# Layer 0's opening by pairs of channel tiles in column groups, with four accumulations begun inside it

## The chip, the cores and the metric

The kernel runs on one core of a Trainium2 chip. The metric is device time in microseconds, the median of three runs. Matrix products run on TensorE (PE), elementwise work on VectorE (DVE) and ScalarE (ACT). SyncE (SP) issues most transfers, ACT some of them, and both draw on the same 16 DMA engines.

## The reference, cut to what matters

The program computes two layers of a hybrid backbone (window attention, convolution and a gated recurrence side by side) over 256 context and 1024 latent tokens of width 1024. What the change touches is how layer 0 begins: the modulation vectors come from `c` and `c_ctx`, the normalised tokens are scaled and shifted by them, and the result `h` (for the context `hc`) feeds every product of the layer.

```python
for l in range(DEPTH):
    shift, scale, gate = jnp.split(jax.nn.silu(c) @ w_ada[l] + b_ada[l], 3, axis=-1)
    shift_c, scale_c, gate_c = jnp.split(jax.nn.silu(c_ctx) @ w_ada[l] + b_ada[l], 3, axis=-1)
    h = layer_norm(x) * (1.0 + scale[:, None]) + shift[:, None]
    hc = layer_norm(ctx) * (1.0 + scale_c) + shift_c
    q, k, v, g_att, u_conv, g_conv, x_lru, g_lru = split_in_proj(h @ w_in[l])
    ...
    g = jax.nn.sigmoid(h @ w_gate + b_gate)
    ...
```

## The kernel before, in words

Everything is float32. A product of tokens and weights is made as three passes: weights and tokens are each split into a high and a low part (`whi`, `wlo`, and `hchi`, `hclo` for the context, `hlhi`, `hllo` for the latent tokens), and high by high, high by low and low by high accumulate in PSUM. The tokens stand as three column groups: NT_C (256 context tokens), NT_0 and NT_1 (512 latent tokens each). The channel axis has eight tiles of 128 (`j` or `k` from 0 to 7), so one output tile of 128 columns over one token group takes 24 matmuls: eight channel tiles by three passes.

`emit_h0` makes layer 0's `h`. `load_ada` brings a 256 by 512 piece of the modulation weights; `ada_rows` multiplies it by the two conditioning vectors in `cs` (two columns of the array) into a row tile `pa`; when a group of 512 columns is complete, `ada_fin` copies it (`arow`), and four small matmuls against `sel` turn it into columns, which DVE adds to the bias in `ada[0]`. Groups 0 and 1 are the shift, 2 and 3 the scale, so the first channel tile can be modulated only when group 2 is done and the last when group 3 is done. `load_x` and `norm_x` bring ten tiles of 128 tokens and normalise them (ACT, `x<-x,nb,rs`). `modulate(j, nt)` transposes one channel tile of a token group on PE (tile `p`), scales and shifts it on ACT (`hf`), and splits it into the high and low parts on ACT and DVE. The order of the loads, row products, normalisations and modulations is a list written out by hand (`order`, line 488). `load_rows` issues eleven small loads of bias and parameter rows on SP's queue, in the middle of the first modulation weights.

After `emit_h0`, `phase1` runs the layer's streams. A planner (`Driver`) picks the next piece among nine streams by priority, with estimates of when engines and operands are free. `lru_in` multiplies `w_in` into the recurrence's input, `gates` multiplies `w_gate` into the merge gates, both through `gemm_nt`, which writes all 24 matmuls of one output tile and then evacuates it. PSUM tiles of the name `ps` come from a ring of four, counted by the pool `pl_`; `gates` may also use wide tiles from another pool, opened after the opening's own. Weights go through `wcols`: a 512 KB load on SP, a copy to `whi` on ACT, a difference to `wlo` on DVE. The compiler's scheduler then orders each engine's queue; a queue runs strictly in that order.

Of the kernel before, what the change touches and what calls it, by code (L numbers as in the profile page):

```python
# [18 lines left out]
KD = 8  # L19
# [170 lines left out]
def kernel(  # L190
# [66 lines left out]
    def load_rows(l, get):  # L257
        ra, rb = get(), get()
        dve.memset(ra[96:128], 0.0)
        dve.memset(rb[96:128], 0.0)  # L260
        for off, n, src in (
            (P_ADA, 24, b_ada[l].rearrange("(r p) -> r p", p=128)),
            (P_GATE, 24, b_gate[l].rearrange("(r p) -> r p", p=128)),
            (P_CB, 4, conv_dw_b[l].rearrange("(r p) -> r p", p=128)),
            (P_CG, 4, conv_ln_g[l].rearrange("(r p) -> r p", p=128)),
            (P_CLB, 4, conv_ln_b[l].rearrange("(r p) -> r p", p=128)),
            (P_LCW, 32, lru_conv_w[l].rearrange("d k (r p) -> (d k r) p", p=128)),
            (P_LCB, 8, lru_conv_b[l].rearrange("d (r p) -> (d r) p", p=128)),
            (P_BA, 8, lru_b_a[l].rearrange("d (r p) -> (d r) p", p=128)),
            (P_BX, 8, lru_b_x[l].rearrange("d (r p) -> (d r) p", p=128)),  # L270
            (P_LAM, 8, lru_lambda[l].rearrange("d (r p) -> (d r) p", p=128)),
        ):
            sp.dma_start(out=ra[off:off + n], in_=src)
        sp.dma_start(out=rb[0:CK * 4], in_=conv_dw_w[l].rearrange("k (r p) -> (k r) p", p=128))
        return ra, rb
# [147 lines left out]
    hT, hr = {}, {}  # L423

# [3 lines left out]

    def emit_h0(R, P):
        tiles = [(ctxt, 0), (ctxt, 128)] + [(x, 128 * i) for i in range(8)]  # L430
        raws, xt = {}, {}
        nts = (NT_C, NT_0, NT_1)

        def load_x(i):
            t = R.tile([128, 2, 512], F32, tag="raw0", name="x0", bufs=17).rearrange("p a b -> p (a b)")
# [3 lines left out]
        def load_ada(g, q):  # L439
            raws[g, q] = R.tile([128, 2, 512], F32, tag="raw0", name="raw0", bufs=17)  # L440
            sp.dma_start(out=raws[g, q], in_=w_ada[0][q * 256:q * 256 + 256, g * 512:g * 512 + 512].rearrange(
                "(k p) n -> p k n", p=128))

        rows_ = {}

        def ada_rows(g, q):
            if q == 0:
                rows_[g] = P.tile([128, 512], F32, tag="p0", name="pa", bufs=4)
            for k in range(2):
                pe.matmul(out=rows_[g][0:2], lhsT=cs[:, q * 2 + k, :], rhs=raws[g, q][:, k, :],  # L450
                          start=(q == 0 and k == 0), stop=(q == 3 and k == 1))
            if q == 3:
                ada_fin(0, [g * 4 + i for i in range(4)], rows_[g], 2,
                        R.tile([128, 512], F32, tag="hf0", name="arow", bufs=5))
# [8 lines left out]
        def modulate(j, nt):  # L463
# [5 lines left out]
            hf = R.tile([128, 512], F32, tag="hf0", name="hf0", bufs=5)  # L469
# [15 lines left out]
        def rows_tile():  # L485
            return R.tile([128, 128], F32, tag="rows", name="rows", bufs=2)

        order = [("a", 0, 0), ("a", 0, 1), ("a", 0, 2), ("r",), ("a", 2, 0), ("a", 0, 3), ("a", 2, 1), ("a", 2, 2),
                 ("a", 2, 3), ("x", 0), ("x", 1), ("a", 1, 0), ("a", 1, 1), ("a", 1, 2), ("a", 1, 3), ("a", 3, 0),
                 ("a", 3, 1), ("a", 3, 2), ("a", 3, 3), ("m", NT_C, 0), ("m", NT_C, 4), ("x", 2), ("x", 3),  # L490
                 ("x", 4), ("x", 5), ("x", 8), ("m", NT_0, 0), ("m", NT_0, 4), ("x", 6), ("x", 9), ("x", 7),
                 ("m", NT_1, 0), ("m", NT_1, 4)]
        for what, *v in order:
            if what == "m":
                for j in range(v[1], v[1] + 4):
                    modulate(j, v[0])
            elif what == "r":
                load_params(0, *load_rows(0, rows_tile))
            elif what == "a":
                load_ada(*v)  # L500
                ada_rows(*v)
            else:
                load_x(*v)
                norm_x(*v)
# [20 lines left out]
    def phase1(l, R, RH):  # L525
# [5 lines left out]
        sl, hl_, pl_ = Pool_(NS), Pool_(NHF), Pool_(4)  # L531
        state = dict(lru=False, late=False)
# [64 lines left out]
        def lru_in():  # L597
            for cc in range(4):
                yield ("pe", both(lambda: xgo[0] >= cc, wroom(), sl.room(), hl_.room(3)))
                w = wcols(w_in[l], O_XL + cc * 128)  # L600
# [18 lines left out]
                for nt in allt:  # L619
                    yield from gemm_nt(w, nt, evac)  # L620
# [482 lines left out]
        gorder = list(range(16, 24)) + list(range(8, 16)) + list(range(8))  # L1103

        def gate_nt(w, j, nt):
# [7 lines left out]
            yield from gemm_nt(w, nt, evac, wide=True)  # L1113
# [3 lines left out]
        def gates():  # L1117
            ws = {}
# [369 lines left out]
```

## Time and profile before

| what | value |
|---|---|
| time, median of 3 runs | 2296.81 us (2293.95 to 2297.31) |
| the profiled execution's own time | 2297.23 us |
| its span, first to last instruction | 2295.4 us |
| PE busy | 2246.4 us (98%) |
| DVE busy | 1680.8 us (73%) |
| ACT busy | 1005.5 us (44%) |
| mean granted clock of TensorE | 0.992 |

PE is busy nearly all the time, so a saving must come from time in which PE waits, works at its lower clock, or does work that need not be done. The views shown below are: the page's list of busy times; stretches of time with the busy time of each engine, the granted clock (1.00 is 2.4 GHz, 0.50 is 1.2 GHz) and the DMA engines' share; groups of instructions with their mean duration; instructions in order of time; and the waits of one engine.

### The profile page before, as it was taken

The page shows a single profiled execution, that of the slowest core. Times are in us where ns is not written, and L with a number is a line of the kernel's source. Part 1 is how long each engine was busy: PE and PEld are TensorE (multiplying, and loading weights), DVE is VectorE, ACT ScalarE, POOL GpSimd, SP SyncE. Part 2 cuts the span into 40 slices and gives each one's busy share as a digit, 9 for nine tenths or more (in the row PEclk, how much of TensorE's full clock was granted, in tenths as well). Part 3 has the DMA queues.
Part 4 walks back from the last instruction along what each step waited for, and adds up shares of the span by engine and source line. Part 5 has one row for each costly group of instructions (what it writes and reads, how often), then busy time and mean ns, then how long its engine had stood idle before and what let it go on. Part 6 is the DMA issues. An engine that isn't in the chain of part 4 may idle for free.

```text
span 2295.4 us, 29965 instructions
## 1 busy us (share of the span) xinstructions
PE 2246.4 (98%) x11344; PEld 1869.6 (81%) x11344; DVE 1680.8 (73%) x2453; ACT 1005.5 (44%) x1642; POOL 88.3 (4%) x140
## 2 busy tenths in 40 slices
PE   7999999999999999999999999999999999999998
PEld 2888888888888787888888888888888878878886
DVE  5579967868859875444668849879778797755667
ACT  3555563245445465421122654565343456642110
POOL 1000000000000110000001200000000011000002
PEclk8999999999999999999999999999999999999999
DMA  7223323433334233545571222224423234347532
GB/s 277 77 74 101 115 68 127 148 106 111 97 114 141 81 104 97 186 165 176 145 229 69 101 61 75 76 91 130 146 87 106 83 115 138 119 145 216 162 127 92
DMA packets 270945, 279.90 MB, mean 122 GB/s; under 512 B 19768, under 2 KB 199888, under 8 KB 270800
## 3 DMA queue, kind: packets, MB, share of 16 engines
q1 hardware_dynamic: 242288, 226.06, 32.0%
q10 hardware_dynamic: 28512, 51.92, 6.4%
q8 instruction: 89, 1.46, 0.3%
q14 instruction: 56, 0.46, 0.1%
HBM read 203.04 MB, written 74.88 MB: 121 GB/s over the span
## 4 chain that ended last, share of the span: by engine, by line
PE 91%; DVE 3%; ACT 2%; DMA 2%; issue 1%; SPq 0%; POOLq 0%; ACTq 0%; DVEq 0%
PE ps L73 84%; PE yp L73 3%; PE pt L73 2%; PE pa L73 1%; DMA raw<-in_w_ada_dram 1%; DMA yst<-yd 1%; ACT whi L73 1%; DVE acc L73 0%; DVE P L73 0%; DVE wlo L73 0%; DVE pl L73 0%; PE p L73 0%; ACT ph L73 0%; DVE gs L73 0%; ACT P L73 0%
## 5 line engine op out<-in xcount | busy, mean ns | idle before, releaser
L73 PE MATMUL ps<-hlhi,whi 128*128 128x512 f32 x1728 | 681.7, 395 | 2.5 <-DVE pl L73 1.5
L73 PE MATMUL ps<-hllo,whi 128*128 128x512 f32 x1728 | 678.0, 392 | 0.0
L73 PE MATMUL ps<-hlhi,wlo 128*128 128x512 f32 x1728 | 677.1, 392 | 0.0
L73 PEld LDWEIGHTS ps<-hlhi,wlo 128*128 128x128 f32 x1728 | 325.8, 189 | 68.1 <-issue 0.4
L73 PEld LDWEIGHTS ps<-hlhi,whi 128*128 128x128 f32 x1728 | 326.2, 189 | 66.5 <-DVE pl L73 2.6
L73 PEld LDWEIGHTS ps<-hllo,whi 128*128 128x128 f32 x1728 | 326.2, 189 | 61.9 <-issue 0.2
L73 DVE SCALAR_TENSOR_TENSOR acc<-u,cwt,acc 128x1296 f32<-128x1296 f32 (+1 forms) x240 | 341.8, 1424 | 2.2
L73 ACT ACTIVATE whi<-raw 128x1024 fp32r<-128x1024 f32 x180 | 190.1, 1058 | 342.3 <-PE ps L73 307.4
L73 DVE TENSOR_TENSOR wlo<-raw,whi 128x1024 fp32r<-128x1024 f32 x180 | 220.5, 1225 | 97.8 <-ACT whi L73 97.4
L73 PE MATMUL ps<-yy,whi 128*128 128x512 f32 (+1 forms) x960 | 271.5, 368 | 1.8 <-DVE m L73 1.8
L73 PEld LDWEIGHTS ps<-yy,whi 128*128 128x128 f32 x960 | 173.6, 188 | 32.5 <-DVE m L73 2.2
L73 PE MATMUL ps<-yy,wlo 128*128 128x512 f32 (+1 forms) x480 | 176.5, 368 | 0.0
L73 ACT ACTIVATE ph<-pt 128x512 fp32r<-128x512 f32 x160 | 94.2, 593 | 146.2 <-PE pt L73 145.6
L73 DVE TENSOR_TENSOR pl<-pt,ph 128x512 fp32r<-128x512 f32 x160 | 109.2, 685 | 60.5 <-ACT ph L73 58.9
L73 PE MATMUL ps<-hchi,whi 128*128 128x256 f32 x480 | 135.9, 283 | 1.5 <-ACT whi L73 0.8
L73 PE MATMUL ps<-hchi,wlo 128*128 128x256 f32 x480 | 135.4, 282 | 1.0 <-DVE wlo L73 1.0
L73 PE MATMUL ps<-hclo,whi 128*128 128x256 f32 x480 | 134.8, 281 | 0.0
L73 ACT ACTIVATE P<-P,nm 128x640 f32<-128x640 f32 (+1 forms) x128 | 101.9, 798 | 72.7 <-DVE nm L73 72.0
L73 DVE CUSTOM_DVE_ANT_0 P<-ps,m_mid,nsink 128x640 f32<-128x640 f32 (+1 forms) x112 | 93.5, 859 | 43.6 <-PE ps L73 42.1
L73 ACT ACTIVATE tg<-ps,drv 128x512 f32<-128x512 f32 (+1 forms) x120 | 76.5, 638 | 68.4 <-PE ps L73 67.9
L73 PEld LDWEIGHTS ps<-yy,wlo 128*128 128x128 f32 x480 | 90.4, 188 | 15.2
L73 PE MATMUL pt<-ident,P 128*128 128x128 f32 x640 | 98.0, 273 | 3.2 <-DVE pl L73 1.4
(205 smaller groups left out, 3398.4 us busy)
## 6 DMA issues: line engine op xcount, KB each, us to landing
raw<-in_w_in_dram SPq DMA_DIRECT2D x60, 512.0 KB
raw<-in_w_ada_dram SPq DMA_DIRECT2D x48, 512.0 KB
raw<-in_w_gate_dram SPq DMA_DIRECT2D x48, 512.0 KB
th<-tg ACTq DMA_DIRECT2D x96, 256.0 KB
thl<-th SPq DMA_DIRECT2D x96, 256.0 KB
yd<-gs ACTq DMA_DIRECT2D x48, 256.0 KB
yst<-yd SPq DMA_DIRECT2D x48, 256.0 KB
raw<-in_w_branch_dram SPq DMA_DIRECT2D x24, 512.0 KB
```

Of the source, the lines that this page charges most:

```text
L73: return f(*a, **k)
```

## The change

Within `emit_h0` the unit of work becomes a pair of channel tiles.

- `load_ada(g)` brings the shift and the scale columns of channel tiles 2g and 2g+1 together, as eight loads of 256 KB with contiguous pieces of 1 KB in DRAM (before: 512 KB with pieces of 2 KB).
- `ada_cols(g)` multiplies them with the conditioning vectors padded to 32 columns (`csz`). The eight channel tiles go to four column groups of the array, `k % 4`, each accumulating two of them into its own 32 partitions of `pa`. ACT copies all 128 partitions, and a matmul against `sel4` (four stacked two-column identities) adds the four partial sums and turns them into columns. The number of matmuls against modulation weights stays 32.
- The weights of the first `lru_in` tile and of the first gate tile are loaded within the opening (`first`), and four accumulations begin there: `lru` over NT_C, NT_0 and NT_1, and `gate` over NT_0. `share(j, nt)` adds channel tile `j` to them: three matmuls each. All four `ps` tiles are held until the planner's streams evacuate them (`pl_.take(4)`).
- The high part's copy is made on ACT for all modulations; before, DVE made it for 10 of 24 (channel tiles 4 to 7 of NT_C and of NT_0, and 6 and 7 of NT_1).
- The eleven small row loads go to ACT's queue.
- The buffers of `x0` and `raw0` become 18 instead of 17, `hf0` 4 instead of 5, and `arow` gets one of its own.

```diff
+        def load_ada(g):
+            for q in range(4):
+                raws[g, q] = R.tile([128, 2, 2, 256], F32, tag="raw0", name="raw0", bufs=18)
+                src = w_ada[0][q * 256:q * 256 + 256, 0:2 * D].rearrange("(k p) (t n) -> p k t n", p=128, t=2)
+                for k in range(2):
+                    sp.dma_start(out=raws[g, q][:, k], in_=src[:, k, :, g * 256:g * 256 + 256])
+        def ada_cols(g):
+            pa = P.tile([128, 512], F32, tag="p0", name="pa", bufs=4)
+            for k in range(KD):
+                c_ = k % 4
+                pe.matmul(out=pa[32 * c_:32 * c_ + 32], lhsT=csz[:, k, :],
+                          rhs=raws[g, k // 2][:, k % 2].rearrange("p t n -> p (t n)"), start=(k < 4), stop=(k >= 4),
+                          tile_position=(0, 32 * c_))
+            row = R.tile([128, 512], F32, tag="arow", name="arow", bufs=1)
+            act.activation(out=row, in_=pa, func=AF.Copy)
+            for i in range(4):
+                pe.matmul(out=pa[:, 2 * i:2 * i + 2], lhsT=row[:, i * 128:i * 128 + 128], rhs=sel4, start=True, stop=True)
...
-            if j < (4, 4, 6)[ti]:
-                act.activation(out=hi, in_=hf[:, 0:n], func=AF.Copy)
-            else:
-                dve.tensor_copy(hi, hf[:, 0:n])
+            act.activation(out=hi, in_=hf[:, 0:n], func=AF.Copy)
...
+        def share(j, nt):
+            for kind in ("lru", "gate"):
+                if (kind, nt[0]) in first:
+                    w, ps = first[kind], first[kind, nt[0]]
+                    for i, (a, b) in enumerate(((0, 0), (0, 1), (1, 0))):
+                        pe.matmul(out=ps[:, 0:nt[2]], lhsT=w[a][:, j, :], rhs=hT[0, nt[0]][b][:, j, :],
+                                  start=(j == 0 and i == 0), stop=(j == KD - 1 and i == 2))
...
+        ra, rb = load_rows(0, lambda: R.tile([128, 128], F32, tag="rows", name="rows", bufs=2), act)
+        for i in range(2):
+            load_x(i)
+        load_ada(0)
...
+        for g in range(1, 4):
+            if g < 3:
+                ada_cols(g + 1)
+            for nt in nts:
+                for j in (2 * g - 2, 2 * g - 1):
+                    share(j, nt)
+                for j in (2 * g, 2 * g + 1):
+                    modulate(j, nt)
+        for nt in nts:
+            for j in (6, 7):
+                share(j, nt)
```

What the change does to the queues is shown at three places. In the rows, `x_214` and `x_216` (before: `x_262`, `x_275`) are the context's token tiles, numbers after a name tell one buffer from another, and `128x512` is the shape written.

PE, the modulation weights. Before, the row products of one piece stand together, two columns wide, and the first transposes come behind three groups of them:

```order
L73 MATMUL pa<-raw_301,cs 2x512 x2
L73 MATMUL pa<-raw_312,cs 2x512 x2
L73 MATMUL p_336<-ident,x_262 128x128
L73 MATMUL p_336<-ident,x_275 128x128
L73 MATMUL p_343<-ident,x_262 128x128
L73 MATMUL p_343<-ident,x_275 128x128
L73 MATMUL pa<-raw_317,cs 2x512 x2
L73 MATMUL pa<-sel,arow 128x2 x4
```

Now:

```order
L73 MATMUL pa<-raw_276,csz 32x512
L73 MATMUL p_419<-ident,x_239 128x128
L73 MATMUL p_428<-ident,x_239 128x128
L73 MATMUL pa<-raw_276,csz 32x512
L73 MATMUL ps<-hchi,wlo 128x256
L73 MATMUL ps<-hchi,whi 128x256
L73 MATMUL ps<-hclo,whi 128x256
L73 MATMUL ps<-hchi,wlo 128x256
L73 MATMUL pa<-raw_279,csz 32x512
```

The matmuls of group 1 are now separated by transposes of the token tiles and by the first shares.

PE, the last modulation weights. Before, they stand ahead of nearly all transposes, and the products with `hchi` begin when those of NT_C are over:

```order
L73 MATMUL pa<-raw_321,cs 2x512 x2
L73 MATMUL pa<-raw_325,cs 2x512 x2
L73 MATMUL p_350<-ident,x_262 128x128
L73 MATMUL p_350<-ident,x_275 128x128
L73 MATMUL pa<-sel,arow 128x2 x4
```

Now they stand behind the whole share of pair 0 and one matmul of pair 1:

```order
L73 MATMUL ps<-hlhi,wlo 128x512
L73 MATMUL ps<-hchi,whi 128x256
L73 MATMUL pa<-raw_407,csz 32x512 x2
L73 MATMUL pa<-raw_410,csz 32x512 x2
L73 MATMUL pa<-raw_413,csz 32x512 x2
L73 MATMUL pa<-raw_416,csz 32x512 x2
L73 MATMUL ps<-hclo,whi 128x256
L73 MATMUL ps<-hchi,wlo 128x256
L73 MATMUL ps<-hchi,whi 128x256
L73 MATMUL p_613<-ident,x_214 128x128
```

All that is left of pair 1's share, and every transpose of pairs 2 and 3, follows the eight matmuls of group 3 in PE's queue.

SP, the transfers. Before, the parameter rows stand behind the first three pieces:

```order
L441 DMA raw_201<-in_w_ada_dram 128x2x512
L273 DMA rows<-in_b_ada_dram 24x128
L273 DMA rows<-in_b_gate_dram 24x128
L273 DMA rows<-in_conv_dw_b_dram 4x128
L273 DMA rows<-in_conv_ln_g_dram 4x128
```

Now SP's queue has none of them in the opening; at its end three weight tiles stand between or behind the last pieces:

```order
L332 DMA raw<-in_w_gate_dram 128x8x128
L449 DMA raw_364<-in_w_ada_dram 128x2x256 x2
L449 DMA raw_367<-in_w_ada_dram 128x2x256 x2
L449 DMA raw_370<-in_w_ada_dram 128x2x256 x2
L449 DMA raw_373<-in_w_ada_dram 128x2x256 x2
L449 DMA raw_407<-in_w_ada_dram 128x2x256 x2
L332 DMA raw<-in_w_gate_dram 128x8x128
L449 DMA raw_410<-in_w_ada_dram 128x2x256 x2
L449 DMA raw_413<-in_w_ada_dram 128x2x256 x2
L449 DMA raw_416<-in_w_ada_dram 128x2x256 x2
L332 DMA raw<-in_w_in_dram 128x8x128
```

The second gate tile is loaded within group 3, and the second `w_in` tile right behind it.

## Rows read from the trace of the kernel before

**Rows 1.** The page, busy time, share of the span and instructions of each engine.
```profile
PE 2246.4 (98%) x11344; PEld 1869.6 (81%) x11344; DVE 1680.8 (73%) x2453; ACT 1005.5 (44%) x1642; POOL 88.3 (4%) x140
```

**Rows 2.** Stretches (us): busy us of PE, PEld, DVE, ACT, POOL; clock, DMA share, GB/s.
```profile
6.40:41.40 35.00, 34.45 (x96) 8.80 (x96) 14.30 (x61) 5.11 (x9) 2.17 (x4) 1.00 0.96 345
41.40:55.40 14.00, 8.14 (x38) 5.62 (x38) 11.88 (x39) 14.00 (x23) 2.29 (x5) 0.62 0.47 162
55.40:58.30 2.90, 2.90 (x15) 2.71 (x14) 2.41 (x6) 2.90 (x5) 1.65 (x2) 0.50 0.70 201
58.30:74.00 15.70, 15.70 (x110) 14.22 (x110) 10.67 (x18) 15.70 (x25) 0.66 (x5) 1.00 0.24 73
...
456.00:600.00 144.00, 135.94 (x765) 115.06 (x764) 113.70 (x206) 69.99 (x145) 0.00 (x0) 0.98 0.36 106
...
790.00:930.00 140.00, 132.41 (x706) 111.15 (x705) 88.22 (x165) 87.66 (x164) 19.54 (x15) 0.96 0.29 90
```

**Rows 3.** Groups of PE's instructions by shape, 0 to 73.97 us: busy, mean ns.
```profile
L73 PE MATMUL pa<-raw,cs 128*2 128x512 f32 x64 | 30.5, 627 | 0.6 <-DMA raw<-in_w_ada_dram 0.3 <-DVE cs L73 0.3
L73 PE MATMUL p<-ident,x 128*128 128x128 f32 x80 | 15.4, 329 | 5.8 <-ACT hf L73 3.9 <-ACT x L73 1.9
L73 PE MATMUL ps<-hchi,whi 128*128 128x256 f32 x16 | 5.1, 320 | 0.0
...
L73 PE MATMUL ps<-hllo,whi 128*128 128x512 f32 x10 | 4.3, 426 | 0.0
L73 PE MATMUL pa<-sel,arow 2*128 2x2 f32 x32 | 4.2, 249 | 0.3 <-ACT arow L73 0.3
...
L73 PE MATMUL ps<-hlhi,wlo 128*128 128x512 f32 x9 | 3.5, 393 | 0.0
```

**Rows 4.** PE in order of time (start, us, operation): how closely matmuls follow each other.
```profile
14.41 7.03 PE L73 MATMUL pa<-raw,cs 128*2 128x512 f32 x16 [0.29 <-DMA raw<-in_w_ada_dram]
...
76.56 0.28 PE L73 MATMUL ps<-hchi,whi 128*128 128x256 f32 x1
...
79.38 0.39 PE L73 MATMUL ps<-hlhi,whi 128*128 128x512 f32 x1
79.61 0.39 PE L73 MATMUL ps<-hllo,whi 128*128 128x512 f32 x1
```

**Rows 5.** The chain of work that ended last, in order of time, near 70 us.
```profile
70.14 0.87 PE p L73 x8
```

**Rows 6.** SP's queue in order of time (start, us, transfers).
```profile
1.91 1.42 SPq L441 DMA_DIRECT2D raw<-in_w_ada_dram  x3
...
9.66 0.25 SPq L274 DMA_DIRECT2D rows<-in_conv_dw_w_dram  x1
```

**Rows 7.** DMA packets and rates in 8:11, 22:30, 33:37 and 39:41.5 us, in this order.
```profile
DMA packets 144, 0.05 MB, mean 18 GB/s; under 512 B 49, under 2 KB 141, under 8 KB 144
...
DMA packets 1605, 3.09 MB, mean 386 GB/s; under 512 B 96, under 2 KB 96, under 8 KB 1605
...
DMA packets 451, 1.63 MB, mean 409 GB/s; under 512 B 55, under 2 KB 55, under 8 KB 450
...
DMA packets 1433, 0.73 MB, mean 294 GB/s; under 512 B 19, under 2 KB 1430, under 8 KB 1433
```

**Rows 8.** Groups of ACT's instructions by shape, 8 to 74 us: busy, mean ns.
```profile
L73 ACT ACTIVATE hf<-p,ada 128x512 f32<-128x512 f32 x15 | 10.8, 757 | 0.0
L73 ACT ACTIVATE hlhi<-hf 128x512 fp32r<-128x512 f32 x10 | 5.8, 613 | 0.0
L73 ACT ACTIVATE whi<-raw 128x1024 fp32r<-128x1024 f32 x4 | 4.2, 1040 | 0.0
L73 ACT ACTIVATE hf<-p,ada 128x256 f32<-128x256 f32 x8 | 4.2, 542 | 0.0
...
L73 ACT ACTIVATE hchi<-hf 128x256 fp32r<-128x256 f32 x4 | 1.5, 398 | 0.0
```

**Rows 9.** Waits of PE, whole span: who waited for whom, us, times, longest.
```profile
PE yp L73 <- ACT ph L73: 7.9, 10, 2.2
```

More of the change, by code (lines that the diff above doesn't have):

```diff
@@ L423 @@
     hT, hr = {}, {}
+    GATES = list(range(16, 24)) + list(range(8, 16)) + list(range(8))
     def alloc_h(ti, n):
@@ new lines, in ada_cols @@
+        def ada_cols(g):
[9 more added lines that the diff above has]
+                pe.matmul(out=pa[:, 2 * i:2 * i + 2], lhsT=row[:, i * 128:i * 128 + 128], rhs=sel4, start=True, stop=True)
+            for part in range(2):
+                jj = 8 * part + 2 * g
+                bias = prm[0][:, P_ADA + jj:P_ADA + jj + 2].unsqueeze(2).to_broadcast([128, 2, 2])
+                dve.scalar_tensor_tensor(out=ada[0][:, jj:jj + 2, :],
+                                         in0=pa[:, 4 * part:4 * part + 4].rearrange("p (m s) -> p m s", s=2),
+                                         scalar=float(part), in1=bias, op0=ALU.add, op1=ALU.add)
@@ L483, in emit_h0 @@
                 pad(H, 64, "padh2")
[L485 to L504, printed above, removed]
+        ra, rb = load_rows(0, lambda: R.tile([128, 128], F32, tag="rows", name="rows", bufs=2), act)
+        for i in range(2):
+            load_x(i)
+        load_ada(0)
+        load_params(0, ra, rb)
+        for i in range(2, 6):
+            load_x(i)
+        for i in range(2):
+            norm_x(i)
+        first["lru"] = wcols(w_in[0], O_XL)
+        load_ada(1)
+        ada_cols(0)
+        for i in range(2, 6):
+            norm_x(i)
+        for i in range(6, 10):
+            load_x(i)
+        first["gate"] = wcols(w_gate[0], GATES[0] * 128)
+        for nt in nts:
+            first["lru", nt[0]] = psum()
+        first["gate", 1] = psum()
+        load_ada(2)
+        for nt in nts:
+            for j in (0, 1):
+                modulate(j, nt)
+            if nt is NT_C:
+                ada_cols(1)
+                load_ada(3)
+            if nt is NT_0:
+                for i in range(6, 10):
+                    norm_x(i)
+        for g in range(1, 4):
+            if g < 3:
+                ada_cols(g + 1)
+            for nt in nts:
+                for j in (2 * g - 2, 2 * g - 1):
+                    share(j, nt)
+                for j in (2 * g, 2 * g + 1):
+                    modulate(j, nt)
+        for nt in nts:
+            for j in (6, 7):
+                share(j, nt)
     class Pool_:
@@ L531, in phase1 @@
         sl, hl_, pl_ = Pool_(NS), Pool_(NHF), Pool_(4)
+        if first:
+            pl_.take(4)
         state = dict(lru=False, late=False)
@@ L598, in lru_in @@
             for cc in range(4):
-                yield ("pe", both(lambda: xgo[0] >= cc, wroom(), sl.room(), hl_.room(3)))
-                w = wcols(w_in[l], O_XL + cc * 128)
+                yield ("pe", both(lambda: xgo[0] >= cc, lambda: "lru" in first or wroom()(), sl.room(), hl_.room(3)))
+                w = first.pop("lru", None) or wcols(w_in[l], O_XL + cc * 128)
                 sl.take()
@@ L619, in lru_in @@
                 for nt in allt:
-                    yield from gemm_nt(w, nt, evac)
+                    if ("lru", nt[0]) in first:
+                        yield "act"
+                        evac(first.pop(("lru", nt[0]))[:, 0:nt[2]], nt)
+                        pl_.give()
+                    else:
+                        yield from gemm_nt(w, nt, evac)
                 w.free()
@@ L1101, in att_out @@
                 yield from gating(0, j, get, 1.0)
-        gorder = list(range(16, 24)) + list(range(8, 16)) + list(range(8))
+        gorder = GATES
         def gate_nt(w, j, nt):
@@ L1111, in evac @@
                 act.activation(out=th[:, 0:nt[2]], in_=ps, func=AF.Tanh, scale=0.5, bias=d[:, 16 + j:17 + j])
-            yield from gemm_nt(w, nt, evac, wide=True)
+            if ("gate", nt[0]) in first:
+                yield "act"
+                evac(first.pop(("gate", nt[0]))[:, 0:nt[2]], nt)
+                pl_.give()
+            else:
+                yield from gemm_nt(w, nt, evac, wide=True)
             act.dma_start(out=th_d[j][:, nt[1]:nt[1] + nt[2]], in_=th[:, 0:nt[2]])
@@ L1117, in gates @@
         def gates():
-            ws = {}
+            ws = {0: first.pop("gate")} if l == 0 else {}
             def fetch(i):
```

34 lines of the change are left out of this document (14 added, 20 removed).

## The prediction

> **What bounds the kernel now.** I read the page's busy times first. PE is busy 2246.4 us of the span [rows 1], so there is little to gain except where PE stands, runs at its lower clock, or does work that is not a product. Next I cut the span into stretches [rows 2]. From 6.4 to 41.4 us PE and the DMA engines are both full (34.45 of 35 us; share 0.96). From 41.4 to 55.4 us PE works 8.14 of 14 us, ACT all of it, and the clock's mean is 0.62. From 58.3 us on PE is full at 1.00.
>
> The question is how late the products of layer 0 start. I call **head** the moment at which the opening is over less the product time already done by then; behind it PE is full, so a shorter head shortens the run by as much, unless later gaps change. Before, the last transposes end at 73.97 us. Until then there are 48 products of 256 columns (three kinds of 16) and 29 of 512 columns (10, 10 and 9) [rows 3]. At full clock one of 256 takes 0.1175 us (24 between 76.56 and 79.38) and one of 512 takes 0.23 us [rows 4]. Done: 48 x 0.1175 + 29 x 0.23 = 12.3 us. The head is 73.97 - 12.3 = **61.7 us**.
>
> What fills it: 64 records against modulation weights (32 matmuls, two records each), 30.5 us of records [rows 3], at 7.03 / 16 = 0.44 us apiece when dense [rows 4]; 80 transposes, in which PE waits 5.8 us for ACT [rows 3]; 32 records against `sel`, 4.2 us; and the lower clock until 58.3 us [rows 2].
>
> **The change, part by part.** The accumulations begun in the opening are 24 x 0.1175 + 72 x 0.23 = 19.4 us of products, 4.85 us for each pair of channel tiles. So the new head is the new end of the opening less 19.4.
>
> *Transfers.* The opening must bring ten token tiles (5.24 MB, pieces of 4 KB), the modulation weights (8.39 MB, now pieces of 1 KB) and three weight tiles that stand ahead of the last piece in SP's queue (first `w_in`, first and second gate tile, 1.57 MB, pieces of 512 B). Pieces of 4 KB moved at 409 GB/s, of 2 KB at 386, of 512 B at 294 [rows 7]. No row shows a full stream of 1 KB pieces, so its rate is bounded by the last two; I take their middle, 340, since 1 KB lies one doubling from each. Sum: 12.8 + 24.7 + 5.3 = 42.8 us (39.8 to 46.6 by the bounds). It starts about 1 us after the first big issue at 1.91 us [rows 6], so at 2.9. The parameter rows leave SP's queue: between 8 and 11 us it moved only 18 GB/s [rows 7] while those issues ran until 9.66 us [rows 6]. That hole of about 3 us goes, but ACT's row loads now share the completion semaphores with SP, which at first has only half of them for pieces of 256 KB; I put 1.5 us back. With 1 us from the last byte to the signal the last modulation weights land at 2.9 + 1.5 + 42.8 + 1 = **48.2 us** (45 to 52).
>
> The Trainium skill says in *DMA: Bandwidth & Descriptors*, Specifications, that line rate needs pieces of at least 512 B. By that the 1 KB pieces would cost nothing against 4 KB, and the modulation weights would take 8.39 / 0.409 = 20.5 us, 4 us less. The rate of 294 GB/s at 512 B [rows 7] speaks against it, and the sum goes by the rows.
>
> *PE behind that landing.* PE's queue is strict, and by the order nearly all of pairs 1 to 3 stands behind the last eight modulation matmuls. What is left then: the last matmul's two records (0.9 us), 40 transposes at 0.87 / 8 = 0.11 us [rows 5] (4.4), eight records against `sel4` (32 took 4.2 us [rows 3], so 1.0) and three pairs of shares (14.6). That is 20.9 us: 48.2 + 20.9 = 69.1 us if PE never waits. I add 3 us for waits of transposes and shares on ACT: before it was 5.8 us with nothing else queued, and now products stand between; bounds 0 and 5.8. I add 2 us for the clock: PE waits for the last weights, and before it regained the full clock 2.9 us after products had become dense at 55.4 (clock 0.50 in 55.4:58.3, 1.00 behind it [rows 2]), which costs half of that; bounds 0 and two such spells with more. The opening ends at **74.1 us**, later than before by nothing to speak of, but with 19.4 us of products done: head 74.1 - 19.4 = **54.7 us**.
>
> *ACT, the other bound.* The new queue holds a copy to `whi` that waits for the second `w_in` tile, 1.8 us of transfer (0.52 MB at 294) behind the last modulation weights: 50 us, then 1.0 for it, and about 1.2 for two late steps. A pair is 2 x (0.54 + 0.40) + 4 x (0.76 + 0.61) = 7.4 us [rows 8], so pairs 2 and 3 end by 52.3 + 14.8 = 67.1 us. PE, at 69.1 to 74.1, is later, so the high copies that ACT takes over from DVE cost nothing; were PE's waits gone, ACT would be next, 2 us earlier.
>
> *The column groups.* At 0.44 us a record one matmul is 0.88 us, a 256 KB piece 0.77 us at 340 GB/s. One after another they lag their data by 8 x 0.11 = 0.9 us a group. Side by side they would free up to 21 us of PE, but in the stretch where PE waits for data. Between the two I take one after another for the end of group 3, and no gain elsewhere.
>
> Speaking against the change, the Trainium skill says in *TensorEngine Tiling (Array Packing)*, Key Properties, that a change of tiling mode drains TensorE. No row here shows a tiled matmul. The order shows 36 such changes in the opening, 35 of them before the last weights are through. A transpose's record lasts 0.27 us beside its 0.11 us share of the queue; if each change exposes that difference, 36 x 0.16 = 5.8 us, of which all but one lie where PE waits for data. The sum stays, but I keep the case below.
>
> *Buffers and the rest.* Group 2 reuses buffers freed by group 0 long before, group 3 those of group 1, whose matmuls are done some 6 us ahead of their issue. SP issues faster than the transfers run (three in 1.42 us [rows 6]). `csz`, `sel4` and the padded copies are a few DVE and ACT steps ahead of the first weights. These I put at nothing; their cover is the wait for the first weights.
>
> *Behind the opening.* The same products remain. The recurrence's first evacuations come earlier, so the planner starts attention earlier in PE's queue. The attention stretches lose time now: 8.1 us of PE gaps in 456:600 and 7.6 in 790:930, with clock means of 0.98 and 0.96 [rows 2], mostly products with values waiting for the split of the transposed scores (7.9 us on `ph`) [rows 9]. Another interleaving can close or open such gaps; the bound is plus or minus 7 us, I take 0.
>
> **Sum:** 61.7 - 54.7 = 7.0 us less. The profiled execution took 2297.23 us, 0.4 above the median; against the median, 2296.81 - 7.0 = **2289.8 us**.
>
> **The rivals.**
> *Full overlap.* The four groups run side by side, the 1 KB pieces move at 386 GB/s, PE keeps its clock, and an earlier start of the recurrence closes a third of the attention gaps: 3 + 2 + 5 us more, about 2280. For it: each bound is open. Against: it needs them all.
> *Eaten up.* PE runs most of the opening at half clock because it waits between small pieces: 14.6 us of shares partly at double time, or every mode change costs 0.16 us and they fall on the path. Head 54.7 + 6 = 60.7, about 2296. For it: the clock fell at 41.4:55.4 when PE worked 58% [rows 2]. Against: three pairs of shares in a row are as dense as 58.3:74 was, at 1.00.
> *Slower.* The planner's new interleaving worsens the attention stretches. They hold 15.7 us of gaps; if these double and the head gains 7, the run takes 2305. It decides from the point where the gaps grow by more than 11.6 us, 4.6 above the gain.
> *The change doesn't do what it says.* The column groups run strictly one after another and drain between, so the grouping saves nothing. The pairing still works; 2290 to 2291, inside the forecast.
>
> **How the numbers follow.** Forecast (2285 to 2294): 0.52, with the case of no real grouping in it. Full overlap: 0.16. Eaten up: 0.20. Slower: 0.12. Ends of the head: transfers -3 to +4, waits -3 to +3, clock -2 to +4, later gaps -7 to +7; taken together about 10 us either side. The range 2279 to 2300 leaves out the better half of the first rival and most of the slower one. A measurement of this kernel can tell about 0.2%, 4.6 us: faster means below 2292.2, slower above 2301.4. Faster: 0.44 of the forecast's 0.52 and all of full overlap, 0.60. Same: the rest of the forecast, eaten up less a little that is slower, 0.26. Slower: 0.14.
>
> **What would show it.** Right: the last modulation weights land near 48 us; PE's products in the first 74 us come to some 19 us; records against modulation weights with 32 columns start either 0.44 us or far less apart; ACT ends its last high copy before PE ends its last share; the attention stretches keep about 15.7 us of gaps. Wrong: a landing behind 53 us, a granted clock of 0.50 beyond 55 us, or PE gaps in the attention stretches that differ by more than 7 us.

## The result, and the profile after

The changed kernel is slower: 2308.1 us (median; 2306.1 to 2309.3) against 2296.1 us for the kernel before in the same session, ratio 1.0052, 95% interval 1.0035 to 1.007. The forecast was 2289.8 us; the time lies above the range. TensorE's busy time is the same to a tenth, 2246.4 us [rows 1], so the 11.4 us that the span grew stand as idle time of PE.

The stretches of [rows 2] in the changed kernel, and the one from 200 to 456 us, which I had not read before; columns as there.

```profile
6.40:41.40 35.00, 26.41 (x72) 7.66 (x72) 19.80 (x82) 13.47 (x19) 3.23 (x6) 0.90 1.02 341
41.40:55.40 14.00, 12.50 (x36) 3.74 (x36) 4.56 (x17) 6.74 (x7) 2.69 (x5) 0.76 0.69 201
55.40:58.30 2.90, 2.81 (x24) 2.45 (x24) 0.97 (x4) 2.90 (x7) 0.00 (x0) 1.00 0.00 0
58.30:74.00 15.70, 15.46 (x103) 12.08 (x102) 10.05 (x18) 15.53 (x30) 0.17 (x3) 1.00 0.26 77
200.00:456.00 256.00, 245.14 (x1301) 206.91 (x1301) 224.64 (x248) 119.94 (x171) 1.04 (x10) 0.98 0.36 114
456.00:600.00 144.00, 143.46 (x818) 122.51 (x817) 108.87 (x183) 71.53 (x138) 0.00 (x0) 1.00 0.35 107
600.00:790.00 190.00, 186.83 (x1076) 159.11 (x1075) 157.24 (x231) 86.41 (x169) 3.28 (x6) 0.99 0.38 118
790.00:930.00 140.00, 130.76 (x709) 110.17 (x708) 83.98 (x159) 85.39 (x158) 18.58 (x15) 0.96 0.29 91
```

Two of these stretches in the kernel before:

```profile
200.00:456.00 256.00, 255.19 (x1365) 215.37 (x1365) 210.90 (x207) 115.45 (x152) 1.10 (x10) 1.00 0.37 118
600.00:790.00 190.00, 189.71 (x1094) 162.54 (x1094) 152.50 (x231) 85.96 (x171) 4.44 (x6) 1.00 0.36 111
```

PE's idle time from 456 to 600 us fell from 8.1 [rows 2] to 0.5 us, but from 200 to 456 it grew from 0.8 to 10.9, from 600 to 790 from 0.3 to 3.2, and from 790 to 930 from 7.6 [rows 2] to 9.2: from 200 to 930 us, 23.8 where there were 16.8. The opening did not win, and from 6.4 to 58.3 us PE was busy for 41.7 of 51.9 us: far more than an engine that mostly waits for data would be.

PE's groups by shape to 77 us, where the last transposes end (compare [rows 3]):

```profile
L73 PE MATMUL pa<-raw,csz 128*32 128x512 f32 x64 | 28.8, 741 | 4.8 <-DMA raw<-in_w_ada_dram 2.7 <-DVE mv L73 1.9 <-ACT hf L73 0.2
L73 PE MATMUL p<-ident,x 128*128 128x128 f32 x80 | 14.7, 294 | 3.0 <-ACT x L73 2.9
L73 PE MATMUL pa<-sel,arow 128*128 128x2 f32 x32 | 4.1, 250 | 1.6 <-ACT arow L73 1.6
```

The 64 records of the modulation cover 28.8 us, against 30.5 before [rows 3]. In order of time (start, us, operation) one sees why; all four lines of the first piece are at full clock:

```profile
33.54 1.05 PE L73 MATMUL pa<-raw,csz 128*32 128x512 f32 x2
34.52 0.44 PE L73 MATMUL p<-ident,x 128*128 128x128 f32 x2
34.89 1.04 PE L73 MATMUL pa<-raw,csz 128*32 128x512 f32 x2
35.86 0.44 PE L73 MATMUL p<-ident,x 128*128 128x128 f32 x2
...
60.41 1.93 PE L73 MATMUL pa<-raw,csz 128*32 128x512 f32 x16 [0.24 <-ACT hf L73]
```

A product that stands alone holds the queue for 0.98 us (34.52 - 33.54). The last eight, in a row, need 1.93 us, where sixteen such records took 7.03 before [rows 4]: the four column groups do run side by side, but only when their products follow one another. And those eight start at 60.41 us. Their data were there at about 50 us: SP had issued the last of them by 43.97 (39.08 + 4.89), the trace has the last completion signal of that transfer at 49.92 us, and in e9 below, where SP issues it at the same time, the engine that waits for it starts at 50.16. From 44 to 49 us the stream moved 331 to 351 GB/s. SP's queue in order of time:

```profile
39.08 4.89 SPq L449 DMA_DIRECT2D raw<-in_w_ada_dram  x6
46.30 0.37 SPq L332 DMA_DIRECT2D raw<-in_w_in_dram  x1
```

The longest wait behind the opening is at 423 us. What PE waited for from 200 to 456 us (who waited for whom, us, times, longest; before there are two waits, of 0.3 us each):

```profile
PE ps L73 <- ACT P L73: 5.1, 1, 5.1
PE ps L73 <- ACT xh L73: 1.9, 1, 1.9
PE ps L73 <- ACT whi L73: 1.2, 1, 1.2
```

VectorE in order of time at that place:

```profile
422.29 1.57 DVE L73 SCALAR_TENSOR_TENSOR acc<-u,cwt,acc 128x1296 f32<-128x1296 f32 x1
423.78 0.75 DVE L73 TENSOR_REDUCE mx<-ps 128x1 f32<-128x256 f32 x2
424.44 1.21 DVE L73 TENSOR_TENSOR wlo<-raw,whi 128x1024 fp32r<-128x1024 f32 x1
425.58 0.15 DVE L73 TENSOR_TENSOR es<-es,sm 128x4 f32<-128x4 f32 x1
425.65 1.56 DVE L73 SCALAR_TENSOR_TENSOR acc<-u,cwt,acc 128x1296 f32<-128x1296 f32 x1
427.13 0.33 DVE L73 TENSOR_SCALAR nm<-mx,nsink 128x1 f32<-128x1 f32 x2
```

PE's score products were done at 422.9 us. Their row maxima (`mx`, `nm`) stand between taps of the convolution (`acc`, 1.56 us each) and a weight split (`wlo`, 1.21 us), so ScalarE's exponential `P` starts at 427.37 and PE at 427.99, at half clock until 437. Before, the first score block comes only behind 60 tap steps, two whole channel tiles; now it comes behind 38.

### The profile page after: what moved, and what is told of

Same layout as the page of the kernel before. It is cut to its first block, busy times and chain, and to the rows that moved or that the text cites. A ratio compares the mean times of both kernels' runs of the same rounds, so it can differ in the third digit from the quotient of the medians.

```text
span 2306.8 us, 29997 instructions
## 1 busy us (share of the span) xinstructions
PE 2246.4 (97%) x11344; PEld 1868.4 (81%) x11344; DVE 1678.6 (73%) x2452; ACT 1012.4 (44%) x1652; POOL 85.4 (4%) x140
## 4 chain that ended last, share of the span: by engine, by line
PE 90%; DVE 5%; ACT 2%; DMA 2%; issue 1%; SPq 0%; POOLq 0%; DVEq 0%; ACTq 0%
PE ps L73 83%; PE yp L73 3%; PE pt L73 3%; DVE acc L73 2%; DMA raw<-in_w_ada_dram 1%; PE pa L73 1%; DMA yst<-yd 1%; DVE P L73 0%; DVE wlo L73 0%; ACT whi L73 0%; PE p L73 0%; ACT L73 0%; DVE pl L73 0%; DMA yd<-gs 0%; ACT P L73 0%
## 5 line engine op out<-in xcount | busy, mean ns | idle before, releaser
L73 PEld LDWEIGHTS ps<-hllo,whi 128*128 128x128 f32 x1728 | 325.9, 189 | 63.5 <-DVE hllo L73 1.6
```

The source lines that it names most:

```text
L73: return f(*a, **k)
```

## The experiments

To compare, I work out two numbers for each profile. The **head**: with each product priced at full clock (0.1175 us for 256 columns, 0.2275 for 512), the time at which products worth 25 us have been issued, less 25. And **idle**: PE's idle time from 200 to 930 us, the length of the four stretches above less PE's busy time in them. Both come from the one profiled execution of a kernel; the times are medians of all its executions, and the kernel before was timed anew in each session. Three profiles of the very same opening (changed, e4, e8) give heads of 62.9, 61.2 and 61.1, so 2 us of a head are noise. The difference between changed and before, 12 us, is 1.1 of head, 7.1 of idle and 3.4 for the clock, since between 85 and 960 us PE ran at half clock for 23.9 us instead of 17.1 and lost half of that. The term for the clock is rough: PE stood still in part of these spells (by its busy time alone they cost 2.4 us more, not 3.4), and a further spell of 3.4 us near 1045 us, which before lacks, adds 1.7.

| kernel | head | idle | time, us | ratio to before (95%) |
|---|---|---|---|---|
| before | 61.7 | 16.8 | 2296 to 2297.5 | 1 |
| changed | 62.9 | 23.8 | 2308.1 | 1.0052 (1.0035, 1.007) |
| e1: opening alone | 63.5 | 16.7 | 2300.9 | 1.0017 (1.0008, 1.0026) |
| e2: column groups alone | 62.5 | 18.6 | 2300.2 | 1.0014 (1.0003, 1.0025) |
| e3: begun accumulations alone | 63.2 | 23.7 | 2307.9 | 1.0047 (1.0034, 1.0059) |
| e4: changed, scores held | 61.2 | 14.9 | 2292.8 | 0.998 (0.9972, 0.9989) |
| e5: e4, high copies divided | 60.6 | 16.9 | 2297.3 | 1.0 (0.9991, 1.0009) |
| e6: e4, whole array | 65.1 | 17.1 | 2300.0 | 1.0018 (1.0009, 1.0027) |
| e7: e3, scores held | 62.9 | 17.0 | 2300.8 | 1.0017 (1.0008, 1.0026) |
| e8: e4, held longer | 61.1 | 34.9 | 2334.4 | 1.0163 (1.0149, 1.0177) |
| e9: e4, products in a row | 52.7 | 14.6 | 2284.0 | 0.9943 (0.993, 0.9957) |
| e10: e5, one swap | 59.8 | 16.6 | 2294.6 | 0.999 (0.9981, 0.9999) |
| e11: e9, high copies divided | 53.4 | 14.2 | 2284.4 | 0.9943 (0.9931, 0.9956) |
| e12: e1, products in a row | 56.1 | 18.8 | 2293.9 | 0.9989 (0.998, 0.9998) |

**The two halves of the change, each alone (e1, e3).** e1 is the changed kernel with these lines of the opening gone, and with them the hand-over of the gate's weights to the planner:

```diff
-        first["lru"] = wcols(w_in[0], O_XL)
-        first["gate"] = wcols(w_gate[0], GATES[0] * 128)
-        for nt in nts:
-            first["lru", nt[0]] = psum()
-        first["gate", 1] = psum()
```

> The changed kernel without the accumulations begun in the opening: no weights fetched there, no shares; pairs, column groups and the parameter rows on ScalarE's queue stay. TensorE's order behind the opening is then nearly that of the kernel before (first score product at row 2146, before 2140, changed 1871). Theory A (two separate causes: the opening wins nothing, and the planner's other interleaving with attention begun among the second channel's taps costs some 10 us near 423 us): no 10 us gap near 423 us, and the time is the kernel before plus what the opening does, 2290 to 2299 us, ratio 0.997 to 1.001. Theory B (the opening alone, its order and its buffers, carries the loss, and the gap near 423 us follows from it): 2305 to 2309 us, as the changed kernel.

e3 is the kernel before with those lines behind its own opening, and the shares behind them:

```diff
+        for nt in nts:
+            for j in range(KD):
+                share(j, nt)
```

> The kernel before with the other part alone: its own opening, then the two weights fetched and all shares of the four begun accumulations issued behind the last modulated tile, so that the planner starts with them done, as in the changed kernel (first score product at row 1865, changed 1871, before 2140; 38 tap steps ahead of the first row maximum, as changed, where before has 60). Theory A (the interleaving alone costs the 10 us): a gap of 4 to 6 us and a half-clock spell of some 10 us near 420 to 440 us, and 2302 to 2309 us. Theory B (the loss comes from the new opening): 2294 to 2299 us, without that gap.

e3 alone costs as much as the whole change (1.0047 against 1.0052), with its old opening. Its longest wait from 200 to 456 us is the same one:

```profile
PE ps L73 <- ACT P L73: 5.1, 1, 5.1
```

In e1 PE is busy 255.19 us of 200 to 456, as before, and its idle time is that of before, 16.7 us. So theory A holds for the large part: the loss comes with the accumulations begun ahead of the planner, whichever opening runs. e1 itself lies 2 us above what A allowed: the new opening alone wins nothing (head 63.5, against 61.7 within the noise), and the time is a little above before.

**Holding the scores (e4, e7, e8).** Every stream behind the opening is placed by the planner, by its estimates of when engines are free, and these come out earlier when the first accumulations are already done. e4 takes away only the early start of attention:

```diff
+                state["taps"] = cc + 1
...
-yield ("act", both(lambda: state["late"] and len(at["proj"]) >= 2 * kv + 2, ...
+yield ("act", both(lambda: state["late"] and (l or state["taps"] >= 2) and len(at["proj"]) >= 2 * kv + 2, ...
```

> The changed kernel with one condition more in the planner: in layer 0 the score blocks may begin only when the convolution has two of its four channel tiles' taps done (56 tap steps ahead of the first row maximum, where the changed kernel has 38 and the kernel before 60). Theory A (the scores begun among the second channel's taps wait on VectorE, and that costs 10 us): the gap near 423 us goes, 2295 to 2301 us. Rival C (a later start only moves the waiting, any other interleaving than the tuned one loses as much): 2304 to 2310 us.

> e3_begun (the opening of before, accumulations begun behind it) with the scores held as in e4_hold. Theory A (the new opening wins nothing, e4_hold is below the kernel before because of the hold and the begun accumulations): 2291 to 2296 us, within 2 us of e4_hold. Rival (the new opening gives some 4 us or more once the later loss is taken away): 2296 to 2300 us.

e8 holds until `state["taps"] >= 3`.

> e4_hold with the score blocks held until three of the four channel tiles' taps are done, not two. Theory A (each score block that runs among the taps waits for VectorE, so fewer of them is better): 2286 to 2291 us. Rival C (the start of before was about right; later the attention lacks time beside the gate products and its waits move to its end, 600 to 930 us): 2295 to 2305 us.

e4 is 15 us faster than the changed kernel, and below the kernel before. The wait for `P` is gone, and with it all of the idle time that the change had added and a little more: 14.9 us, against 23.8 with the early start and 16.8 before; PE's half clock between 85 and 960 us is back at 17.1 us. Less idle by 8.9, 3.4 for the clock and 1.7 of head make 14 of the 15 us. Rival C was wrong for two channel tiles but right for three: in e8 the attention lacks time, and its waits move to 563 us and later.

```profile
PE pt L73 <- ACT P L73: 7.7, 1, 7.7
...
PE yp L73 <- DVE pl L73: 5.8, 6, 2.6
PE ps L73 <- DVE m L73: 5.7, 1, 5.7
```

e7 mends e3 likewise, by 7 us, but ends 8 us above e4: theory A is out, and the time lies 0.8 us beyond the far end of the rival's range. With the scores held, then, the kernel with the new opening is the faster one, but only 1.7 us of the 8 show in the head, no more than its noise; 2.1 are idle time, 1.7 are the distance of the two profiled executions from their medians, and most of the rest is clock (see *What stays open*).

**What the column groups give (e2, e6).** e2 puts the groups into the old opening:

```diff
-                pe.matmul(out=rows_[g][0:2], lhsT=cs[:, q * 2 + k, :], rhs=raws[g, q][:, k, :],
-                          start=(q == 0 and k == 0), stop=(q == 3 and k == 1))
+                c_ = (q * 2 + k) % 4
+                pe.matmul(out=rows_[g][32 * c_:32 * c_ + 32], lhsT=csz[:, q * 2 + k, :], rhs=raws[g, q][:, k, :],
+                          start=(q < 2), stop=(q >= 2), tile_position=(0, 32 * c_))
```

> The kernel before with one part of the change: the modulation's products in four column groups of the array (128 partitions x 32 columns of c, of which 2 are not zero, the four partial rows summed by a selection matrix of 128 x 2), in the old order of loads with 512 columns a piece, two of the eight products at a time. Nothing else is changed and the planner's order stays. The 64 records of the modulation took 27.5 us of TensorE in the opening of before; in the changed kernel pairs of such products took 1.05 us for 4 records and sixteen records 1.93 us. Theory A (TensorE, in its strict order, bounds the opening): the 64 records fall to 8 to 15 us, the transposes end 6 to 12 us earlier, and the time is 2284 to 2290 us. Rival (the modulation's products wait for the transfers or ScalarE's copies end the opening anyway): 2292 to 2297 us.

The rival named the reason, but its range was too low by 3 us: e2 is even a little slower than before. Its PE groups from 0 to 74 us, and two stretches of [rows 2]:

```profile
L73 PE MATMUL pa<-raw,csz 128*32 128x512 f32 x64 | 17.4, 911 | 1.8 <-DMA raw<-in_w_ada_dram 1.4 <-DVE csz L73 0.5
...
L73 PE MATMUL p<-ident,x 128*128 128x128 f32 x80 | 16.3, 345 | 7.5 <-ACT x L73 4.0 <-ACT hf L73 2.7 <-DVE ada L73 0.7
```

```profile
6.40:41.40 35.00, 26.44 (x114) 10.09 (x114) 14.78 (x65) 9.45 (x18) 2.24 (x4) 0.74 0.94 352
41.40:55.40 14.00, 8.54 (x32) 6.15 (x32) 12.52 (x40) 12.80 (x18) 3.29 (x7) 0.50 0.64 181
```

The modulation gave back 13 us of PE's records (from the 30.5 of [rows 3]; the 27.5 of the expectation was too low). But the token tiles came little earlier (ACT normalised the last one by 60.6 us, before by 63.4), the transposes waited 7.5 us instead of 5.8 [rows 3], most of it for ACT's `x`, and PE, now with gaps, ran at 0.74 and 0.50 of its clock where before it had 1.00 and 0.62 [rows 2]. I read from this that in the old order PE's work on the modulation was hidden beside the transfers.

e6 takes the groups out of e4 (products of 2 columns through the whole array):

```diff
-                pe.matmul(out=pa[32 * c_:32 * c_ + 32], lhsT=csz[:, k, :], ..., start=(k < 4), stop=(k >= 4),
-                          tile_position=(0, 32 * c_))
+                pe.matmul(out=pa[0:2], lhsT=cs[:, k, :], ..., start=(k == 0), stop=(k == KD - 1))
```

> e4_hold without the column groups: the eight products of a pair's modulation accumulate in one bank through the whole array, with 2 columns of c, and the selection is over 2 rows. Everything else as in e4_hold. Theory A (the groups save only where products stand in a row, 5 us of TensorE in the last pair alone, beside a ScalarE that is the bound there): 2291 to 2296 us. Rival (the groups carry the opening, the sum of the 64 records doubles): 2298 to 2304 us.

The rival again, though nothing doubles: the records rise from 27.0 to 34.8 us and the head by 3.9, of 7.2 us of time. In the new opening the records are on the path.

```profile
L73 PE MATMUL pa<-raw,cs 128*2 128x512 f32 x64 | 34.8, 668 | 5.5 <-DVE nb L73 3.5 <-DMA raw<-in_w_ada_dram 2.0
```

**ScalarE in the opening (e5).**

```diff
-            act.activation(out=hi, in_=hf[:, 0:n], func=AF.Copy)
+            if j < (4, 4, 6)[ti]:
+                act.activation(out=hi, in_=hf[:, 0:n], func=AF.Copy)
+            else:
+                dve.tensor_copy(hi, hf[:, 0:n])
```

> The changed kernel with the scores held as in e4_hold, and the high copies of the opening divided as in the kernel before (VectorE takes them from channel tile 4 on, 6 in the last token tile) instead of all on ScalarE. In the changed kernel ScalarE's 20 last modulations and their copies run one after another from 54.2 to 79 us. Theory A (ScalarE ends the changed opening): 10 copies less there, 4 x 0.42 and 6 x 0.63 us, so 4 to 6 us less than e4_hold's 2292.8: 2287 to 2289 us. Rival (TensorE's strict order ends it, as I first read the trace, or VectorE becomes as late): within 1.5 us of e4_hold, 2291 to 2295 us.

The head moved by 0.6 us, so ScalarE is not the bound. The time nevertheless rose by 4.5 us, 2.0 of them idle behind 200 us, which neither theory had (the rest under *What stays open*).

**One swap (e10).** One dependence of order, no other edit:

```diff
+            if wcount[0] == 78:
+                tc.add_manual_dep(i_.ins, yts[-3], ...NoSync...)
```

> e5_hold_hi with two instructions of VectorE swapped near 810 us, nothing else: one weight's low part (1.22 us) is pinned behind the join of an attention block (yt), as it stands in the kernel before and in e4_hold, where the compiler's list put it ahead in e5_hold_hi, e1, e2, e6 and e7. In all five of these TensorE has a gap of 2.2 us there, waiting for yt, and a half-clock spell of 3.4 us behind it. Theory A (this swap is what puts e5_hold_hi 4.5 us above e4_hold): no gap near 810 us, 2291 to 2294.5 us. Rival (the difference comes from elsewhere, chance from run to run or the half-clock spells): 2295.5 to 2299 us.

VectorE near 808 us in e5 and in e10:

```profile
808.35 1.22 DVE L73 TENSOR_TENSOR wlo<-raw,whi 128x1024 fp32r<-128x1024 f32 x1
809.48 0.85 DVE L73 TENSOR_TENSOR yt<-yp,yt 64x256 f32<-64x256 f32 x2
```

```profile
808.10 0.86 DVE L73 TENSOR_TENSOR yt<-yp,yt 64x256 f32<-64x256 f32 x2 [0.53 <-issue]
808.99 1.22 DVE L73 TENSOR_TENSOR wlo<-raw,whi 128x1024 fp32r<-128x1024 f32 x1
```

PE's gap there fell from 2.2 to 1.6 us only, and the time by 2.7 us, just outside what theory A allowed, with intervals that overlap; the profile of e10 is also of the fastest of its eleven executions (2291.1 us). The expectation was wrong on one point: of the five kernels that it names, all have the gap of 2.2 us, but only e1, e5 and e7 have a spell of half clock right behind it. It is not settled: such swaps may be worth some microseconds, and comparisons between my kernels are no finer than 3 to 4 us where their orders differ in the attention.

**The products in a row (e9, e12, e11).** A copy of the padded c, made behind the pair's last transfer, keeps all eight back until they can go together:

```diff
+            pool.tensor_scalar(out=z, in0=raws[g, 3][:, 1, 1, 255:256], scalar1=0.0, scalar2=None, op0=ALU.mult)
+            pool.tensor_tensor(out=cg, in0=csz, in1=z.unsqueeze(2).to_broadcast([128, KD, 32]), op=ALU.add)
...
-                pe.matmul(out=pa[32 * c_:32 * c_ + 32], lhsT=csz[:, k, :],
+                pe.matmul(out=pa[32 * c_:32 * c_ + 32], lhsT=cg[:, k, :],
```

> e4_hold with one dependence more: the eight products of a pair's modulation read a copy of the padded c that GpSimd makes behind the pair's last transfer (plus zero times one of its elements), so that TensorE has all eight in a row. In e4_hold they stand one or two at a time between transposes and shares, and a product that stands alone takes 1.0 us at full clock and 1.9 at half, four groups or not; in a row sixteen records took 1.93 us. Theory A (TensorE's strict order, lengthened by singly issued products, bounds the opening): the 64 records fall from 28 us to 8 to 15 us of TensorE, the head at equal product work from 61.2 to 52 to 57 us, and the time from 2292.8 to 2284 to 2289 us. Rival (the last transfers of x and ScalarE bound it as well, or waiting for the last of eight transfers costs what the row saves): head 60 to 63, 2291 to 2296 us.

> e1_no_begun (pairs and column groups, no begun accumulations, the planner's order as before) with the eight products in a row as in e9_row. Theory A (what the row gives stands by itself, 8 to 9 us as between e4_hold and e9_row): 2300.85 falls to 2291 to 2293.5 us, head from 63.5 to 54 to 56; the rest to e9_row's 2284 is then what the begun accumulations with the hold give. Rival (without shares TensorE has nothing to put between the products, they stood in a row more often and the order was not the bound): 2295 to 2300 us.

e9's products in order of time:

```profile
16.46 3.64 PE L73 MATMUL pa<-raw,cg 128*32 128x512 f32 x16 [1.48 <-POOL cg L457]
...
29.77 3.64 PE L73 MATMUL pa<-raw,cg 128*32 128x512 f32 x16 [0.17 <-POOL cg L457]
...
42.93 1.92 PE L73 MATMUL pa<-raw,cg 128*32 128x512 f32 x16
...
51.47 1.92 PE L73 MATMUL pa<-raw,cg 128*32 128x512 f32 x16 [0.47 <-POOL cg L457]
```

GpSimd's step that waits for a pair's last transfer, for the last pair:

```profile
50.16 0.21 POOL L456 TENSOR_SCALAR z<-raw 128x1 f32<-128x1 f32 x1 [7.42 <-DMA raw<-in_w_ada_dram]
```

The products' group, and the stretches to 74 us:

```profile
L73 PE MATMUL pa<-raw,cg 128*32 128x512 f32 x64 | 11.1, 830 | 2.1 <-POOL cg L457 2.1
```

```profile
6.40:41.40 35.00, 18.41 (x81) 9.69 (x81) 25.12 (x96) 18.07 (x24) 7.18 (x14) 0.80 1.04 343
41.40:55.40 14.00, 13.54 (x98) 8.85 (x96) 7.32 (x12) 13.45 (x24) 2.47 (x5) 1.00 0.79 236
55.40:58.30 2.90, 2.90 (x18) 2.50 (x17) 1.45 (x3) 1.90 (x5) 0.00 (x0) 1.00 0.69 196
58.30:74.00 15.70, 15.70 (x102) 13.82 (x102) 5.75 (x11) 11.48 (x21) 1.01 (x10) 1.00 0.03 7
```

Theory A, in full: the records fall to 11.1 us, the head to 52.7, and 2284.0 us beats both kernels. PE is now idle while the transfers run (18.41 us busy of 35), and the last eight products start at 51.47 us instead of 60.41, 1.3 us behind the signal that their data are there (50.16). The two rows of 3.64 us ran at half speed: the one at 29.77 lies in a half-clock spell (23.9 to 34.2 us), while the clock's own record shows none at 16.46. e9 takes away two things at once, the products issued alone and most of the changes of tiling mode (8 instead of 36); no run separates them. e12 shows the same step without begun accumulations: head 63.5 to 56.1, time down by 7.0, to 0.4 us above what was expected.

> e9_row with the high copies of the opening divided between ScalarE and VectorE as in the kernel before. In e5_hold_hi that moved the head at equal product work by half a microsecond only, while TensorE's order was the bound. Theory A (with the products in a row ScalarE, busy 42.9 to 69 us with the modulations and their copies, is the next bound): head 52.7 falls to 48 to 51, 2279 to 2282.5 us. Rival (TensorE is still the bound, or VectorE, which then has copies and low parts, is as late): 2282.5 to 2288 us.

In e11 ScalarE works 8.31 us from 58.3 to 74 instead of 11.48 and nothing is won: PE's own queue, nearly full from 41.4 us on, is the bound as far as the rows show.

```profile
58.30:74.00 15.70, 15.70 (x102) 13.76 (x101) 8.20 (x18) 8.31 (x13) 1.17 (x10) 1.00 0.04 8
```

## Why the prediction was wrong, step by step

- *Transfers: right.* 340 GB/s and a landing at 48.2 us (45 to 52) were forecast; 331 to 351 GB/s and 49.9 us came. No run shows by themselves the 1.5 us that I put back for ACT's row loads or the 1 us from the last byte to the signal; the 49.9 us contain them. The Trainium skill says in *DMA: Bandwidth & Descriptors*, Specifications, that line rate needs pieces of at least 512 B; by that I had estimated 4 us less for pieces of 1 KB. The measurement differs, since pieces of 4 KB had 409 GB/s [rows 7].
- *PE behind that landing: the size right, the start wrong.* I put 20.9 us of PE's work behind the last weights; from 60.41 us to the last shares, near 84, it was about 22, with 2 us of the planner's products between them that don't count. The step that failed is the sentence that the column groups and the mode changes rest on, "in the stretch where PE waits for data". PE waited for modulation weights for 2.7 us in the whole opening and for the last eight not at all: it came 10.5 us late to them (60.41 against 49.92). The three earlier groups cost 27 us of records, issued one or two at a time, and transposes and shares stood between them in the strict queue. I had the durations (0.88 us a product, one after another) and 36 changes of tiling mode, and laid both beside a wait that they used up. Moved into a row, the same products give a head of 52.7, where the sum had 54.7. With PE in time for the data the head is about what was forecast; that it is so near is in part luck, since in e9 the products also run side by side, which the sum did not have, and PE idles more while the transfers run.
- *Column groups: wrong in both ways.* I took "one after another for the end of group 3, and no gain elsewhere". Side by side they take 1.93 us for the sixteen records of group 3, and taken away from all groups they cost 3.9 us of head (e6).
- *Mode changes.* The Trainium skill says in *TensorEngine Tiling (Array Packing)*, Key Properties, that a change of tiling mode drains TensorE. The trace agrees in kind: from 33.54 to 34.89 us one product and two transposes take 1.35 us, where the dense rows give 0.88 + 0.22 [rows 4, 5], so by this estimate about 0.12 us a change. That is near the 0.16 I weighed; 36 of them are 4 us, and they lay on the path, not beside a wait. It was my rival "eaten up" that came nearest to the opening, at 60.7 forecast and 62.9 measured. It had the mode changes on the path, but not the products issued alone, so part of its nearness is luck.
- *ACT: right in its price.* Its high copies cost nothing (e5, e11). Its end was forecast at 67.1 us (from 52.3, which by its own terms is 52.2) and came at 79.3, since its modulations waited for PE's late transposes.
- *Waits and clock.* I allowed 3 + 2 us behind the landing. Behind 60.41 us neither came: PE was busy 15.46 of 15.70 us from 58.3 to 74, at full clock. They came earlier: to 74 us PE idled 4.0 us more than before, and it fell to half clock from 24.2 to 31.0 and from 41.3 to 48.1 us, as long in all as before (13.6 us, from 44.7 to 58.3).
- *Behind the opening: the term taken as 0 was about 10.5 us (7.1 idle, 3.4 clock).* I had seen that attention would start earlier, and bounded its price by 7 us from the gaps of 456 to 600 and 790 to 930 us. Those two together shrank by 5.9 us, so the sign that I had named for this (a change of more than 7 us there) did not show the loss; nor did either of my other two signs of being wrong appear in the opening. The price arose where before had no gap at all, from 200 to 456 us, because VectorE was still at work on the convolution there (busy 224.64 of 256 us). Rows of idle time in the old order could not show it; VectorE's row could have: 210.90 of those 256 us busy already, with 1.56 us steps, and a score block that needs its row maxima at once. The rival "slower" had the kind of mechanism, with too little chance and in the wrong place. That its time (2305) is nearly right is luck: it took 7 us of gain in the head, which didn't come, and 15.7 us of added gaps, of which 7.1 came.

Together: the opening gave -1.1 instead of 7.0 us, 8.1 us short, and the rest lost 10.5; together 18.6, where the forecast missed by 18.3 (2308.1 - 2289.8).

**What stays open.** 2 to 4 us by which the medians of e5, e6 and e7 lie above what head and idle time say against e4 are not in the table. Between the profiled executions (e4 2294.0 us; e5 2297.3, e6 2299.2, e7 2300.3) the clock accounts for most of it. All three have a spell of 3.4 us at half clock near 1035 us that e4 lacks, up to 1.7 us each, and e6 has 6.9 us less of half clock between 85 and 960 us. Head, idle time and clock then give 3.1, 4.3 and 5.6 us above e4, where 3.4, 5.3 and 6.3 were measured. Just ahead of that spell PE waits for 2.1 to 2.5 us in these three, and for 2.0 in e4; why the clock fell in the three alone is open. The orders of e5, e6 and e7 also differ from e4's by few rows in the attention; e10 names one candidate and doesn't prove it.

## What to carry to other kernels

Before work is placed "beside a wait", see whether the engine's own strict queue reaches the wait at all: add up what stands ahead of it in the queue, and compare with the landing. Column groups paid here only for products that follow one another; keep such products back until the whole row can go. Where a planner sets the order, an early finish at the start is a new input to every later decision: look for the first place at which another stream now starts, and read how full the engines that it needs are there, gaps or no gaps.

## What the runs showed of the hardware

- Four fp32 products of 128 x 32 against 512 columns in four column groups run at the same time: sixteen records in 1.93 us at full clock (3.64 us in a half-clock spell, e9), 3.6 times as fast as the 7.03 us of products issued one after another through the whole array [rows 4]; alone between other instructions each takes 0.98 us.
- Less work on PE beside the same transfers was not faster: with 17.4 instead of 30.5 us of modulation records PE's clock fell to 0.74 from 6.4 to 41.4 us (e2), and its other work, the transposes (16.3 against 15.4 us [rows 3]) and the selections (5.8 against 4.2 us [rows 3]), took longer.
- The stream of mostly 1 KB pieces moved 331 to 351 GB/s from 44 to 49 us in the changed kernel, between the 294 of 512 B and the 386 of 2 KB [rows 7].
